# Forget and gate columns computed behind the value columns, in blocks of 344 to 358, in a two-layer decoder trunk

## The chip, the cores and the metric

The kernel runs on one core of a Trainium2 chip. The metric is device time of one execution in microseconds; the time before is the median of three runs, 2304.24 (2301.83 to 2304.35). Less is better.

## The reference, cut to what matters

A token sequence of 256 x 2048 passes through two layers in float32. Each layer normalises the residual stream, projects it with one combined matrix, runs attention, projects back, adds, and then does the same with a squared-ReLU MLP (2048 to 8192 to 2048).

```python
# layer 0: combined projection, split into
qa, ka, va, ga, fa, qd, kd, vd = split(h @ w_in)    # 1024 x 4, 8, 1024 x 3 columns
log_f = log_sigmoid(fa + b_f)                       # 8 forget columns, one for each head
o_a = fox_attention(qa, ka, va, log_f) * sigmoid(ga)
# layer 1: combined projection, split into
q, kc, vc, ks, vs, kw, vw, gt = split(h @ w_in)     # 2048, 512 x 6, 48 columns
gates = sigmoid(gt)                                 # 3 gates for each of 16 heads
kc, vc = compress(kc), compress(vc)                 # flat blocks of 32 tokens @ w1, gelu, @ w2
o = gate0 * o_cmp + gate1 * o_slc + gate2 * o_win   # three attention branches a head
```

With 256 tokens there are only four selection blocks, so the selected branch takes every block and is an ordinary causal attention.

## The kernel before, in words

Tokens lie on partitions in two halves of 128. Every float32 product is made of three matmuls: activations and weights are each split into a high and a low part, and high x high, high x low and low x high are summed in PSUM. The transposed activations xT are kept on chip in both parts; the weights are streamed.

A block of the input projection is 512 weight columns wide: `in_proj` (line 662) calls `a_units` (line 271). The 16 slices of the inner dimension come in four chunks of four (1 MB, one DMA on the SP queue; three raw buffers), and each chunk is two units of 1024 columns (two slices of 512). For each unit, ScalarE copies the high part (line 235) and VectorE subtracts to get the low part (line 236). `ahead` (line 250) writes out the split of the unit three places on, and the load of the next chunk, before each unit's matmuls; a load waits until the chunk that had its buffer is split. A unit of 512-column slices has 12 matmuls, with xT as the weights of the array and the streamed columns as the moving operand. The last unit ends with an evacuation of either half from PSUM (`plain` at line 665, or `Prep.evac` for q and k, which adds the norm).

The narrow columns, 8 forget columns in layer 0 and 48 gate columns in layer 1, have a unit of their own, `t_units` (line 363): one chunk of all 16 slices; the narrow weights are held by the array and xT moves (16 pairs of matmuls of 512 and 256 columns, lines 373 and 374). The sum is then turned by two small transposes (line 384), and `evac_fa` (line 650) or `evac_gt` (line 839) does the pointwise part.

All instructions of an engine run in the order written. The order is set by a small planner, `Background` (line 104 on): heads, norms and transposes are tasks that advance step by step in "slots", which the main matmuls offer four times a unit (`yield`; two steps at most a slot). Steps of one kind are held apart by a number of slots, also across tasks:

```python
APART = {"s": 4, "t": 3, "o": 5, "d": 3}   # scores, transposes, values, scaling
```

`bg.need(task)` runs slots with no main matmul between them until the task is done (forced slots). Three such places matter here. `phi_units` (line 863), the compression's first product, forces the task that transposes the tokens and adds position terms (`bg.need(tok[kind], ...)`, line 870; the task is started as the token block's last half is evacuated). `out_proj` (line 730) forces, unit by unit, the two heads whose rows it is to multiply (`odd_ready`, line 1039). And q and k evacuations of layer 0's dilated heads force the heads whose buffers they overwrite.

The order of blocks in layer 0 is: q, k, forget unit, v, gate (output gate) for heads 0 to 3; q, k, v, gate for heads 4 to 7; then q, k, v for each group of four dilated heads. A group's four head tasks start when its v block is evacuated. In layer 1 it is: k tokens, gate unit, phi for k (two chunks), v tokens, ks, phi for v, kw, vs, q0, vw, q1, q2, q3, output projection. A group of four heads (and its compressed-branch task `odd_comp`) starts when its q block is evacuated; each head has two "s", two "t" and one "o" step, `odd_comp` one "s" and one "t", and the preparation of q ("Prep") two "d" and three "t". A head holds two of eight score tiles.

Of the kernel before, what the change touches and what calls it, by code (L numbers as in the profile page):

```python
# [12 lines left out]
AF = mybir.ActivationFunctionType  # L13
ALU = mybir.AluOpType
AX = mybir.AxisListType

S = 256
# [130 lines left out]
def trunk_kernel(ctx: ExitStack, tc: tile.TileContext, x, w_up, w_down, even_w_in, even_w_out,  # L148
# [58 lines left out]
    def weight_chunk(w, k0, nk, segs):  # L207

        width = sum(n for _, n in segs)
        pieces, at = [], 0  # L210
        for c0, n in segs:
            src = w[k0 * 128:(k0 + nk) * 128, c0:c0 + n].rearrange("(k p) c -> p k c", p=128)
            pieces.append((nk, width, at, n, src))
            at += n
        return chunk(pieces)
# [144 lines left out]

                units.append((ci, j0 * 512, 1024, gen, True))

    def t_units(w, c0, m, rhs, evac, pre):

        ci = weight_chunk(w, 0, KT, [(c0, m)])

        def gen(u):
            pre(range(KT))
            o = rotate("main", bank[0:3])[:m]
            h = wh[u % NHL][:, :KT * m].rearrange("p (k c) -> p k c", c=m)  # L370
            lo = wl[u % NHL][:, :KT * m].rearrange("p (k c) -> p k c", c=m)
            for k in range(KT):
                nc.tensor.matmul(o, h[:, k], rhs(k), start=k == 0, stop=False)
                nc.tensor.matmul(o[:, :S], lo[:, k], rhs(k)[:, :S], start=False, stop=k == KT - 1)
                if k % 4 == 3 and k < KT - 1:
                    yield
            a, b = T[8][:m, 0:S], T[8][:m, S:2 * S]
            nc.scalar.activation(a, o[:, S:], AF.Copy)
            nc.vector.tensor_tensor(b, o[:, :S], a, ALU.add)

            def turn():
                t = rotate("tp", bank[3:5])
                for hf in range(2):
                    nc.tensor.transpose(t[:, hf * m:(hf + 1) * m], b[:, hf * 128:(hf + 1) * 128], ident[:m, :m])
                for hf in range(2):
                    evac(hf, t[:, hf * m:(hf + 1) * m])
                yield 2
            turned.append(bg.spawn(turn(), 4))
            yield

        units.append((ci, 0, KT * m, gen, True))

    turned = []


    class Norm:
        def __init__(self, name, gain):
# [59 lines left out]
    def rotate(name, of):  # L457
        rot[name] += 1
        return of[(rot[name] - 1) % len(of)]
# [202 lines left out]
    def in_proj(segs, evac, norm, nk=4):  # L662
        return a_units(W, segs, xl, list(range(KT)), evac, main3, norm.need, nk=nk)

    def plain(norm, dst, then=None):
        def evac(hf, ps):
            nc.scalar.activation(dst[:, hf * 512:(hf + 1) * 512], ps, AF.Copy, scale=norm.rows()[:, hf:hf + 1])
            if hf == 1 and then:
                then()
        return evac  # L670

    def even_head(kind, i, head, qT, kT, v, preps, gate):
        yield (lambda: all(p.task and p.task.done for p in preps) and turned[0].done and free_ht), "s"
        t = free_ht.pop(0)
        s = rotate("s", bank[5:7])
        if kind == "fox":
            scores(s, qT, kT, lambda tt, p: nlf[p][:, tt, head:head + 1].to_broadcast([128, 128]))
        else:
            scores(s, qT, kT)
        softmax(s, c_("mask") if kind == "fox" else c_("lc"), SM[t], stat[t])  # L680
        yield 8, "t"
        transposed(SM[t], SM[t])
        yield 7
        yield (lambda: gate is None or gate and gate[0].task and gate[0].task.done), "o"
        o = bank[7][:, (head % 2) * 256:(head % 2) * 256 + 256]
        values(o, v, i, SM[t], True, True)
        parts(head, o, gate and gate[0].dst[:, i * S:(i + 1) * S])
        free_ht.append(t)

    W = even_w_in  # L690
    qs = [T[0], T[1]]
    nblk = 0
    for kind, base, h0 in (("fox", 0, 0), ("dil", 4 * FOX_W + 8, 8)):
        for blk in range(2):
            qT, kT, v = (T[2], T[3], T[6]) if nblk % 2 == 0 else (T[4], T[5], T[7])
            nblk += 1
            preps = []
            for j, (dst, nm) in enumerate(((qT, "q"), (kT, "k"))):
                def evac(hf, ps, j=j, dst=dst, nm=nm, preps=preps, kind=kind, blk=blk):
                    if hf == 0:  # L700
                        n0.rows()
                        if kind == "dil":
                            bg.need(*[heads[blk * 4 + i] for i in range(4)])
                        if kind == "fox":
                            p = Prep(n0, qs[j], dst, cols["fox"] if nm == "q" else None, None)
                        else:
                            p = Prep(n0, qs[j], dst, cols[nm + "d"], rt[nm + "d"])
                        preps.append(p)
                    preps[j].evac(hf, ps)
                in_proj([(base + j * FOX_W + blk * 512, 512)], evac, n0)  # L710
            if nblk == 1:
                t_units(W, 4 * FOX_W, 8, xr, evac_fa, n0.need)

            gate = [] if kind == "fox" else None

            def then(kind=kind, blk=blk, h0=h0, qT=qT, kT=kT, v=v, preps=preps, gate=gate):
                for i in range(4):
                    head = h0 + blk * 4 + i
                    heads[head] = bg.spawn(even_head(kind, i, head, qT[:, i * S:(i + 1) * S], kT[:, i * S:(i + 1) * S], v, preps, gate), 1 + i)
            in_proj([(base + 2 * FOX_W + blk * 512, 512)], plain(n0, v, then), n0)  # L720

            if kind == "fox":
                def gate_evac(hf, ps, blk=blk, gate=gate):
                    if hf == 0:
                        gate.append(Gate(n0, qs[0], T[8 + blk]))
                    gate[0].evac(hf, ps)
                in_proj([(3 * FOX_W + blk * 512, 512)], gate_evac, n0)
# [201 lines left out]

    def odd_comp(g, qT, prep):  # L930

        yield (lambda: prep[0].task and prep[0].task.done and comp["k"].done and comp["v"].done and turned[1].done), "s"
        b = rotate("s", bank[5:7])[:, 0:128].rearrange("p (f h n) -> p f h n", f=2, h=4)
        c, st = cs, cst[g % 2]
        for hf in range(2):
            for h in range(4):
                nc.tensor.matmul(b[:, hf, h, 0:NCMP], qT[:, h * S + hf * 128:h * S + (hf + 1) * 128], kcT[:, g],
                                 start=True, stop=True, skip_group_check=True)
        cv = c[:, :, :, 0:NCMP]

        def bc(name):
            return c_(name).rearrange("p (f n) -> p f n", f=2)[:, :, None, :].to_broadcast([128, 2, 4, NCMP])

        def per(at):
            return st[:, at:at + 8].rearrange("p (f h) -> p f h", f=2)

        nc.vector.tensor_tensor(cv, b[:, :, :, 0:NCMP], bc("mc"), ALU.add)
        nc.vector.tensor_reduce(per(0), cv, AX.X, ALU.max)
        nc.vector.tensor_tensor(cv, cv, per(0)[:, :, :, None].to_broadcast([128, 2, 4, NCMP]), ALU.subtract)
        nc.scalar.activation(cv, cv, AF.Exp)  # L950
        nc.vector.tensor_tensor(cv, cv, bc("m01"), ALU.mult)
        nc.vector.tensor_reduce(per(0), cv, AX.X, ALU.add)
        nc.vector.tensor_scalar(st[:, 0:8], st[:, 0:8], 1e-30, None, op0=ALU.max)
        nc.vector.reciprocal(st[:, 0:8], st[:, 0:8])
        gt = gates.rearrange("p f (h b) -> p f h b", b=3)[:, :, 4 * g:4 * g + 4, 0]
        nc.vector.tensor_tensor(per(0), per(0), gt, ALU.mult)
        nc.vector.tensor_tensor(cv, cv, per(0)[:, :, :, None].to_broadcast([128, 2, 4, NCMP]), ALU.mult)
        yield 10, "t"
        t = rotate("tp", bank[3:5])
        for hf in range(2):  # L960
            nc.tensor.transpose(t[:, hf * 128:(hf + 1) * 128], c[:, hf].rearrange("p h n -> p (h n)"), ident)
        nc.scalar.activation(pcT[g % 2], t[:, :S], AF.Copy)
        yield 4
# [34 lines left out]
        in_proj([(c0, 512)], plain(n1, src, then), n1)  # L998

    comp_block("k", Q_W)  # L1000
    t_units(W, Q_W + 6 * KV_W, 48, xr, evac_gt, n1.need)
    phi_units("k", k_w1)
    comp_block("v", Q_W + KV_W)

# [25 lines left out]
        in_proj([(g * 512, 512)], evac, n1)  # L1030

    k_block("w", Q_W + 4 * KV_W, kwT, "okw")
    in_proj([(Q_W + 3 * KV_W, 512)], plain(n1, vs), n1)
    q_block(0)
    in_proj([(Q_W + 5 * KV_W, 512)], plain(n1, vw, lambda: vdone.append(True)), n1)
    for g in range(1, 4):
        q_block(g)

    def odd_ready(ks):
# [59 lines left out]
```

## Time and profile before

| | us |
|---|---|
| median of three runs | 2304.24 |
| profiled execution | 2303.22 |
| its span, first to last instruction | 2301.4 |
| TensorE busy | 2285.3 |
| VectorE busy | 1382.1 |
| ScalarE busy | 1086.6 |

Busy times are sums over the span; TensorE's include overlaps of matmuls that follow each other, so the cost of one is read from the start of one to the start of the next. In rows in order of time the columns are start, duration (both us), engine, line, operation, output and input tiles with their forms, and how many were merged; a square bracket at the end gives idle time before the instruction and what released it. The granted clock is TensorE's, with 1.00 as full speed.

### The profile page before, as it was taken

Reading aid. Unit: us, or ns where it says so; the run is one execution under the profiler, and the core shown is the slowest. Engines: PE = TensorE matmul, PEld = TensorE weight load, DVE = VectorE, ACT = ScalarE, POOL = GpSimd, SP = SyncE. Lnnn points to the kernel's source line nnn. Section 1 sums busy time; section 2 is a strip of 40 time slices with the busy share of each in tenths; the row PEclk is TensorE's granted clock in tenths of the full one; section 3 lists DMA queues with packets and bytes.
Section 4 is the critical chain, followed back from the end, with each engine's and each line's share of the span. In section 5 each row is a group of like instructions: output and inputs, shape, how many; then the busy total and the mean of one; then the engine's idle time right before and its main releaser. Section 6 shows DMA issues by size and latency. Waiting matters only on the chain.

```text
span 2301.4 us, 28635 instructions
## 1 busy us (share of the span) xinstructions
PE 2285.3 (99%) x11399; PEld 1922.5 (84%) x11399; DVE 1382.1 (60%) x2075; ACT 1086.6 (47%) x1573; POOL 30.0 (1%) x28
## 2 busy tenths in 40 slices
PE   8999999999999999999999999999999999999999
PEld 6788888888888888888888888788888888888887
DVE  5565655666566566566654666766666556566564
ACT  5554554544444444444443555555544444444342
POOL 0000000000000000000000000000000000000000
PEclk9999999999999999999999999999999999999999
DMA  6555555555555565565546653335555565555654
GB/s 240 165 165 171 176 165 167 181 192 193 184 198 186 188 196 183 183 201 184 188 148 204 215 165 121 118 110 174 191 186 190 181 199 193 187 193 176 203 195 148
DMA packets 212694, 414.47 MB, mean 180 GB/s; under 512 B 10705, under 2 KB 11985, under 8 KB 212561
## 3 DMA queue, kind: packets, MB, share of 16 engines
q1 hardware_dynamic: 211552, 411.53, 54.9%
q8 instruction: 89, 1.46, 0.3%
q10 hardware_dynamic: 1008, 1.12, 0.1%
q14 instruction: 45, 0.36, 0.0%
HBM read 410.52 MB, written 2.10 MB: 179 GB/s over the span
## 4 chain that ended last, share of the span: by engine, by line
PE 96%; DVE 1%; ACT 1%; DMA 1%; issue 0%; POOL 0%; ACTq 0%; POOLq 0%
PE bank L311 34%; PE bank L340 21%; PE bank L337 11%; PE bank L300 8%; PE bank L298 8%; PE bank L299 8%; PE bank L616 1%; PE bank L588 1%; PE bank L611 1%; DMA raw<-in_even_w_in 1%; PE bank L876 1%; DVE wl L236 1%; PE bank L507 1%; PE bank L617 0%; PE bank L425 0%; PE bank L584 0%
## 5 line engine op out<-in xcount | busy, mean ns | idle before, releaser
L236 DVE TENSOR_TENSOR wl<-raw,wh 128x1024 fp32r<-128x1024 f32 (+1 forms) x772 | 937.9, 1219 | 768.5 <-ACT wh L235 766.3
L235 ACT ACTIVATE wh<-raw 128x1024 fp32r<-128x1024 f32 (+1 forms) x772 | 812.3, 1054 | 864.8 <-PE bank L311 324.1
L340 PE MATMUL bank<-xT,wh 128*128 128x512 f32 x2048 | 707.6, 397 | 0.0
L337 PE MATMUL bank<-xT,wl 128*128 128x256 f32 x2048 | 543.0, 281 | 0.0
L340 PEld LDWEIGHTS bank<-xT,wh 128*128 128x128 f32 x2048 | 371.5, 188 | 75.2
L337 PEld LDWEIGHTS bank<-xT,wl 128*128 128x128 f32 x2048 | 386.6, 189 | 18.5
L311 PE MATMUL bank<-wh,big 128*128 128x512 f32 x1280 | 358.8, 391 | 0.0
L311 PE MATMUL bank<-wh,xT 128*128 128x512 f32 x1156 | 325.6, 395 | 0.8 <-ACT xT L430 0.7
L311 PEld LDWEIGHTS bank<-wh,big 128*128 128x128 f32 x1280 | 239.6, 188 | 49.3 <-DVE big L625 0.2
L298 PE MATMUL bank<-wh,big 128*128 128x512 f32 x640 | 252.8, 395 | 0.0
L311 PEld LDWEIGHTS bank<-wh,xT 128*128 128x128 f32 x1156 | 214.9, 188 | 44.6 <-ACT xT L430 1.3
L300 PE MATMUL bank<-wh,big 128*128 128x512 f32 x640 | 249.5, 390 | 0.0
L299 PE MATMUL bank<-wl,big 128*128 128x512 f32 x640 | 249.2, 389 | 0.0
L311 PE MATMUL bank<-wl,big 128*128 128x512 f32 x640 | 202.8, 393 | 0.0
L311 PE MATMUL bank<-wl,xT 128*128 128x512 f32 x578 | 188.5, 397 | 0.0
L300 PEld LDWEIGHTS bank<-wh,big 128*128 128x128 f32 x640 | 120.1, 188 | 25.7 <-DVE big L625 0.4
L298 PEld LDWEIGHTS bank<-wh,big 128*128 128x128 f32 x640 | 120.4, 188 | 24.4 <-ACT big L624 0.2
L311 PEld LDWEIGHTS bank<-wl,big 128*128 128x128 f32 x640 | 120.2, 188 | 24.5
L299 PEld LDWEIGHTS bank<-wl,big 128*128 128x128 f32 x640 | 120.4, 188 | 23.5
L311 PEld LDWEIGHTS bank<-wl,xT 128*128 128x128 f32 x578 | 108.5, 188 | 22.5 <-DVE wl L236 0.2
L787 DVE SCALAR_TENSOR_TENSOR xs<-bank,r_m,xs 128x512 f32<-128x512 f32 x128 | 89.9, 743 | 7.8 <-PE bank L300 7.8
L773 ACT ACTIVATE big<-t 128x256 fp32r<-128x256 f32 x128 | 52.5, 415 | 81.9 <-DVE t L769 81.9
(179 smaller groups left out, 1454.9 us busy)
## 6 DMA issues: line engine op xcount, KB each, us to landing
raw<-in_w_up SPq DMA_DIRECT2D x128, 1024.0 KB, 5.3
raw<-in_w_down SPq DMA_DIRECT2D x128, 1024.0 KB, 5.1
raw<-in_even_w_in SPq DMA_DIRECT2D x55, 1024.0 KB, 5.1
raw<-in_odd_w_in SPq DMA_DIRECT2D x40, 1024.0 KB, 5.1
raw<-in_even_w_out SPq DMA_DIRECT2D x16, 1024.0 KB, 5.0
raw<-in_odd_w_out SPq DMA_DIRECT2D x16, 1024.0 KB, 5.3
out_x<-xs SPq DMA_DIRECT2D x8, 256.0 KB, 2.5
xs<-in_x SPq DMA_DIRECT2D x3, 512.0 KB, 8.8
```

The costliest lines, as they stand in the source:

```text
L235: nc.scalar.activation(h, r, AF.Copy)
L236: nc.vector.tensor_tensor(lo, r, h, ALU.subtract)
L298: nc.tensor.matmul(o, lhs(k, 0, hf), h[:, n], start=st, stop=False)
L299: nc.tensor.matmul(o, lhs(k, 0, hf), lo[:, n], start=False, stop=False)
L300: nc.tensor.matmul(o, lhs(k, 1, hf), h[:, n], start=False, stop=last and n == len(ks) - 1)
L311: nc.tensor.matmul(bks[hf], lhs(k, part, hf), w_[:, n], start=False, stop=False)
L337: nc.tensor.matmul(o[:, :S], lo[:, n, j * 128:(j + 1) * 128], rhs(k)[:, :S], start=False, stop=last and n == 1)
L340: nc.tensor.matmul(o, h[:, n, j * 128:(j + 1) * 128], rhs(k), start=first and n == 0, stop=False)
L507: nc.tensor.transpose(b[:, i * S + hf * 128:i * S + hf * 128 + 128], self.src[:, hf * 512 + h * 128:hf * 512 + (h + 1) * 128], ident)
L588: nc.tensor.matmul(s[:, 128:384], qT[:, 128:256], kT, start=True, stop=bias is None, skip_group_check=True)
L773: nc.scalar.activation(d[:, k, 0], q_, AF.Copy)
L787: nc.vector.scalar_tensor_tensor(xd, ps, norm.r2[:, hf:hf + 1], xd, op0=ALU.mult, op1=ALU.add)
```

## The change

`t_units` is gone. `rows_block` takes a list of column ranges, lays them side by side, cuts the total into three blocks of equal, even width, and computes each as an ordinary block of `in_proj`. A block that spans two ranges loads each chunk in two DMAs and evacuates each piece with its own function. In layer 0 the 1024 value columns of heads 0 to 7 and the 8 forget columns make 1032, three blocks of 344; they stand behind the first k block, where the forget unit and the first v block were, and the second v block is gone from its place. Heads 0 to 3 start when the third block is evacuated, heads 4 to 7 when their k block is. In layer 1 the 512 vs, 512 vw and 48 gate columns make 1072, blocks of 358, 358 and 356; they stand where vs stood, and q0 to q3 follow one another. The gate unit between the k tokens and phi is gone.

```diff
-    def t_units(w, c0, m, rhs, evac, pre):
...
+    def rows_block(norm, sources, count, then):
+        places, n = [], 0
+        for c0, m, take in sources:
+            places.append((n, n + m, c0, take))
+            n += m
+        step = -(-n // count) + (-(-n // count)) % 2
+        for i in range(count):
+            cut = [(max(a, i * step), min(b, (i + 1) * step), a, c0, take) for a, b, c0, take in places
+                   if a < (i + 1) * step and b > i * step]
+
+            def evac(hf, ps, i=i, cut=cut):
+                for a, b, base, _, take in cut:
+                    take(hf, a - base, ps[:, a - i * step:b - i * step])
+                if hf == 1 and i == count - 1:
+                    then()
+            in_proj([(c0 + a - base, b - a) for a, b, base, c0, _ in cut], evac, norm)
+
+    def kept(norm, dst):
+        def take(hf, a, ps):
+            d = dst[:, hf * 512 + a:hf * 512 + a + ps.shape[-1]]
+            nc.scalar.activation(d, ps, AF.Copy, scale=norm.rows()[:, hf:hf + 1])
+        return take
...
+                    if hf == 1 and j == 1 and kind == "fox" and blk == 1:
+                        then()
                 in_proj([(base + j * FOX_W + blk * 512, 512)], evac, n0)
-            if nblk == 1:
-                t_units(W, 4 * FOX_W, 8, xr, evac_fa, n0.need)
...
-            in_proj([(base + 2 * FOX_W + blk * 512, 512)], plain(n0, v, then), n0)
+            if kind == "dil":
+                in_proj([(base + 2 * FOX_W + blk * 512, 512)], plain(n0, v, then), n0)
+            elif blk == 0:
+                def fa_then(then=then):
+                    fa_done.append(True)
+                    then()
+                rows_block(n0, [(2 * FOX_W, 512, kept(n0, T[6])), (2 * FOX_W + 512, 512, kept(n0, T[7])),
+                                (4 * FOX_W, 8, lambda hf, a, ps: evac_fa(hf, ps))], 3, fa_then)
...
     comp_block("k", Q_W)
-    t_units(W, Q_W + 6 * KV_W, 48, xr, evac_gt, n1.need)
     phi_units("k", k_w1)
...
     k_block("w", Q_W + 4 * KV_W, kwT, "okw")
-    in_proj([(Q_W + 3 * KV_W, 512)], plain(n1, vs), n1)
-    q_block(0)
-    in_proj([(Q_W + 5 * KV_W, 512)], plain(n1, vw, lambda: vdone.append(True)), n1)
-    for g in range(1, 4):
+    VS, VW = Q_W + 3 * KV_W, Q_W + 5 * KV_W
+    rows_block(n1, [(VS, KV_W, kept(n1, vs)), (VW, KV_W, kept(n1, vw)), (VW + KV_W, 48, lambda hf, a, ps: evac_gt(hf, ps))],
+               3, lambda: vdone.append(True))
+    for g in range(4):
         q_block(g)
```

The waits on the turned forget and gate columns (`turned[0].done`, `turned[1].done`) become waits on the third block's evacuation.

## Rows read from the trace of the kernel before

**Rows 1.** The page: busy time by engine, and the chain that ended last, by engine.
```profile
PE 2285.3 (99%) x11399; PEld 1922.5 (84%) x11399; DVE 1382.1 (60%) x2075; ACT 1086.6 (47%) x1573; POOL 30.0 (1%) x28
...
PE 96%; DVE 1%; ACT 1%; DMA 1%; issue 0%; POOL 0%; ACTq 0%; POOLq 0%
```

**Rows 2.** TensorE in order of time, around the forget unit of layer 0.
```profile
59.14 0.39 PE L299 MATMUL bank<-wl,xT 128*128 128x512 f32 x1
...
61.64 0.39 PE L373 MATMUL bank<-xT,wh 128*8 128x512 f32 x1
...
67.19 0.40 PE L298 MATMUL bank<-wh,xT 128*128 128x512 f32 x1
...
69.02 0.39 PE L300 MATMUL bank<-wh,xT 128*128 128x512 f32 x1
...
69.55 0.50 PE L298 MATMUL bank<-wh,xT 128*128 128x512 f32 x1
```

**Rows 3.** The same view, ten microseconds on: a transpose of k.
```profile
77.19 0.55 PE L507 MATMUL bank<-ident,t 128*128 128x128 f32 x3 [0.43 <-DVE t L492]
```

**Rows 4.** Groups of instructions: the splits (count, busy us, mean ns, idle before).
```profile
L236 DVE TENSOR_TENSOR wl<-raw,wh 128x1024 fp32r<-128x1024 f32 x766 | 934.0, 1224 | 765.4 <-ACT wh L235 763.3
L235 ACT ACTIVATE wh<-raw 128x1024 fp32r<-128x1024 f32 x766 | 808.9, 1058 | 863.1 <-PE bank L311 322.4 <-PE bank L340 320.9 <-PE bank L300 188.5
```

**Rows 5.** ScalarE in order of time: first forget instruction, first split behind them.
```profile
71.15 0.21 ACT L656 ACTIVATE stat<-stat 128x8 f32<-128x8 f32 x1 [2.44 <-DVE stat L654]
...
75.83 2.94 ACT L235 ACTIVATE wh<-raw 128x1024 fp32r<-128x1024 f32 x3
```

**Rows 6.** DMA issues: output, input, queue, count, KB each, median us to landing.
```profile
raw<-in_even_w_in SPq DMA_DIRECT2D x55, 1024.0 KB, 5.1
...
raw<-in_odd_w_in SPq DMA_DIRECT2D x1, 384.0 KB, 5.5
...
raw<-in_even_w_in SPq DMA_DIRECT2D x1, 64.0 KB, 5.1
```

**Rows 7.** All engines in order of time, from the k tokens' block to phi.
```profile
1189.86 21.57 SPq L227 DMA_DIRECT2D raw<-in_odd_w_in  x4
...
1195.67 0.39 PE L300 MATMUL bank<-wh,xT 128*128 128x512 f32 x1
...
1196.10 0.69 ACT L667 ACTIVATE t<-bank,r_a 128x512 f32<-128x512 f32 x1 [0.61 <-PE bank L300]
...
1197.29 0.60 PE L855 MATMUL bank<-ident,t 128*128 128x128 f32 x4
1197.64 0.47 PE L373 MATMUL bank<-xT,wh 128*48 128x512 f32 x1
...
1199.59 1.22 DVE L236 TENSOR_TENSOR wl<-raw,wh 128x1024 fp32r<-128x1024 f32 x1 [9.76 <-ACT wh L235]
...
1200.73 2.48 DVE L859 TENSOR_TENSOR t<-bank,vecs 128x512 f32<-128x512 f32 x4
...
1202.67 3.81 PE L876 MATMUL bank<-t,raw 128*128 128x60 f32 x32 [0.20 <-DVE t L859]
```

**Rows 8.** TensorE in order of time, from group 1's transposes to head 7's values.
```profile
1404.83 0.60 PE L507 MATMUL bank<-ident,t 128*128 128x128 f32 x4
...
1450.89 0.39 PE L298 MATMUL bank<-wh,big 128*128 128x512 f32 x1
...
1467.56 0.60 PE L588 MATMUL bank<-t,t 128*128 128x256 f32 x2
1470.51 0.96 PE L985 MATMUL bank<-pcT,t 128*128 128x256 f32 x2 [2.35 <-DVE big L625]
```

**Rows 9.** Stretches: busy us (count) of five engines, granted clock, DMA share, GB/s.
```profile
75.00:80.00 5.00, 4.57 (x26) 3.56 (x24) 3.98 (x7) 4.24 (x6) 0.00 (x0) 1.00 0.00 0
...
1470.00:1472.50 2.50, 1.99 (x6) 1.68 (x7) 1.66 (x10) 0.99 (x4) 0.00 (x0) 0.66 0.00 0
1472.50:1475.00 2.50, 2.50 (x12) 2.09 (x11) 0.64 (x2) 0.39 (x1) 0.00 (x0) 0.66 0.00 0
1475.00:1480.00 5.00, 5.00 (x29) 4.25 (x28) 2.77 (x10) 3.15 (x7) 0.00 (x0) 1.00 0.01 3
...
1471.00:1472.00 1.00, 1.00 (x4) 0.81 (x3) 0.20 (x3) 0.74 (x4) 0.00 (x0) 0.50 0.00 0
```

More of the change, by code (lines that the diff above doesn't have):

```diff
@@ L361, in b_units @@
                 units.append((ci, j0 * 512, 1024, gen, True))
-    def t_units(w, c0, m, rhs, evac, pre):
[L365 to L393, printed above, removed]
     class Norm:
@@ L670, in plain @@
         return evac
+    def rows_block(norm, sources, count, then):
[18 more added lines that the diff above has]
+        return take
     def even_head(kind, i, head, qT, kT, v, preps, gate):
-        yield (lambda: all(p.task and p.task.done for p in preps) and turned[0].done and free_ht), "s"
+        yield (lambda: all(p.task and p.task.done for p in preps) and fa_done and free_ht), "s"
         t = free_ht.pop(0)
@@ L692, in trunk_kernel @@
     nblk = 0
+    fa_done = []
     for kind, base, h0 in (("fox", 0, 0), ("dil", 4 * FOX_W + 8, 8)):
@@ L697, in trunk_kernel, with then, evac @@
             preps = []
+            gate = [] if kind == "fox" else None
+            def then(kind=kind, blk=blk, h0=h0, qT=qT, kT=kT, v=v, preps=preps, gate=gate):
+                for i in range(4):
+                    head = h0 + blk * 4 + i
+                    heads[head] = bg.spawn(even_head(kind, i, head, qT[:, i * S:(i + 1) * S], kT[:, i * S:(i + 1) * S], v, preps, gate), 1 + i)
             for j, (dst, nm) in enumerate(((qT, "q"), (kT, "k"))):
-                def evac(hf, ps, j=j, dst=dst, nm=nm, preps=preps, kind=kind, blk=blk):
+                def evac(hf, ps, j=j, dst=dst, nm=nm, preps=preps, kind=kind, blk=blk, then=then):
                     if hf == 0:
@@ L709, in evac @@
                     preps[j].evac(hf, ps)
+                    if hf == 1 and j == 1 and kind == "fox" and blk == 1:
+                        then()
                 in_proj([(base + j * FOX_W + blk * 512, 512)], evac, n0)
-            if nblk == 1:
-                t_units(W, 4 * FOX_W, 8, xr, evac_fa, n0.need)
[L714 to L719, printed above, removed]
-            in_proj([(base + 2 * FOX_W + blk * 512, 512)], plain(n0, v, then), n0)
+            if kind == "dil":
[6 more added lines that the diff above has]
+                                (4 * FOX_W, 8, lambda hf, a, ps: evac_fa(hf, ps))], 3, fa_then)
             if kind == "fox":
@@ L930, in odd_comp @@
     def odd_comp(g, qT, prep):
-        yield (lambda: prep[0].task and prep[0].task.done and comp["k"].done and comp["v"].done and turned[1].done), "s"
+        yield (lambda: prep[0].task and prep[0].task.done and comp["k"].done and comp["v"].done and vdone), "s"
         b = rotate("s", bank[5:7])[:, 0:128].rearrange("p (f h n) -> p f h n", f=2, h=4)
```

## The prediction

> **What bounds the kernel now.** I read the page first: the busy shares, then the chain that ended last [rows 1]. TensorE is busy for 2285.3 of 2301.4 us and carries 96% of the chain, so a microsecond is gained where a TensorE column goes, and lost where TensorE stands still. Then I read TensorE in order of time around the two column units that go (forget and gate), and last the three places where its work could come to depend on what stood around them: the first compression, the ScalarE chain behind the forget columns, and the sixteen odd heads before their output projection.
>
> What a matmul costs is read from start to start, since the durations overlap. From 59.14 to 61.64 stand 11 matmuls of 512 columns: 0.2273 us each. From 61.64 to 67.19 stand the forget unit's 16 pairs of 512 and 256 columns: 0.3469 a pair, so 0.1196 for 256 [rows 2]. A straight line through the two is 0.4207 ns a column and 0.012 us beside it: 0.1566 for 344, 0.1625 for 358, 0.1617 for 356. The bounds are the plain proportions from either side: for 344, 0.1527 (from 512) and 0.1607 (from 256).
>
> **The change part by part.**
>
> *Layer 0, columns.* Out go two value blocks of 96 matmuls (192 x 0.2273 = 43.64) and the forget unit (5.55). In come 3 x 96 matmuls of 344: 45.10 (43.98 to 46.28 by the bounds). That is -4.09. The unit's two transposes go as well (from 69.02 to 69.55 passes 0.53 where a matmul takes 0.23: -0.30), and with them a stop of 0.43 at 77.19, where a transpose waited for VectorE behind the forget arithmetic [rows 2, 3]. Together -4.8.
>
> *Layer 1, columns.* 43.64 + 5.55 + 0.30 go; 96 x (2 x 0.1625 + 0.1617) = 46.72 come (45.7 to 48.1). That is -2.8. Both: -7.6, with -9.7 and -5.0 as ends.
>
> The Trainium skill, "TensorE: Matmul & The Clock Gate", section "Back-to-back issue gap", puts the start-to-start time at columns/2.4 ns plus a fixed 2.5 ns. By it both layers' matmuls would save about 7.6 against my 6.6 from the rows alone, and the forecast below would be 1.0 lower. The rows show 227 ns for 512 columns where the rule gives 216, so I keep the rows.
>
> *Splits and evacuations.* 48 units of 688 or 716 columns replace 32 of 1024 and two small ones. A 1024-column unit takes ScalarE 1.058 and VectorE 1.224 [rows 4], beside 12 matmuls of 2.73; in proportion the narrow ones take about 0.7 and 0.85 beside 1.88 to 1.95. Cover stays, cost nothing. The forget arithmetic moves into the evacuation. Before, ScalarE was held by it from 71.15 to 75.83 [rows 5]; this now starts at the end of the third block, when three gate units of 2.73 are already split: 8.2 us plus the block's last half of 0.9, against some 6.5 for the chain and 2.3 for the next split. Cost nothing, 0.5 if it is missed.
>
> *Loads.* The pieces are narrower and most chunks have two. The 64 KB forget chunk of 2048 rows of 32 B landed in 5.1 us like a 1024 KB chunk, the 384 KB gate chunk in 5.5 [rows 6]; a quarter of these rows comes with each chunk of the third block. A chunk can be issued some eight units (15 us) before its own unit, so 6 to 7 us for two pieces are covered. The Trainium skill, "DMA: Bandwidth & Descriptors", section "Specifications", puts line rate at 512 B and more and so speaks against pieces of 32 and 192 B; by it loads would be late, which is rival D.
>
> *The first compression (layer 1).* The step that I find most costly. Before, the 48-column unit stood between the k tokens' block and the phi matmuls, and hid that the tokens must be evacuated, transposed and given their position terms. Now `phi_units` forces that task at once (line 870). Worked out on the rows of before [rows 7]: TensorE's last matmul of the block starts at 1195.67, so it is free at 1195.90; evacuation runs from 1196.10 to 1196.8, and the transposes followed it at 1197.29. Four of them passed in 0.35 (to 1197.64), so eight end at 1198.0. VectorE has the split of the second unit of the v tokens ahead of the additions: ScalarE copies after the evacuation (1196.8 to 1197.85), VectorE subtracts to 1199.1; then four additions of 0.62 (the row's 2.48), of which the phi matmuls need three: 1200.96, start at 1201.05. TensorE is idle for 1.4 + 3.0 = 4.4 us. Before it stood 0.2 at this place, so +4.2. The queue of loads adds nothing: the v tokens' first load goes out one place earlier than at 1189.86. Bounds: 1.3 if the additions came before the split and ran beside the transposes, 6 if the evacuation too is queued behind a split that waits for its load.
>
> *The clock after it.* The nearest rows: after TensorE stood still for 2.35 us before 1470.51, its granted clock was 0.50 from 1471 to 1472, the lower of its two levels (1.2 for 2.4 GHz). The two rows from 1470 to 1475 have 0.66, the next 1.00: 5 x 0.34 / 0.5 = 3.4 us at half speed, 1.7 us of work lost [rows 8, 9]. A stop of 3.0 should cost the same: +1.7 (0 to 1.7).
>
> *The odd heads.* q0 moves behind the value blocks, so vw's 32 slots no longer lie between q0 and q1. By my count of planner slots, nine steps of kind "s" a group at four slots are 36, where one block has 32. Before, group 0 had 64 slots ahead of group 1, whose q transposes began at 1404.83, behind group 0's last values. Still head 7 was late when the output projection, begun at 1450.89, asked for it: the 2.35 us before 1470.51 [rows 8]. After, group 1's transposes take turns with group 0's ("t", three slots), and its prep ends some 17 slots later. Heads 4 and 5, wanted by the projection's third unit, are then some 20 slots short, 6 and 7 a further 7. Forced slots carry head work that is needed anyway (three scores, five transposes, two heads' values: about 7 us), and ScalarE and VectorE need some 9.8 for the same steps: one more stop of about 2.5. Bounds 0 and 8.7 (below). I take +2.5, nearest to the 2.35 of the row. The last two groups run under forced slots too and so gain the room back before the second pass.
>
> *Sum*: -7.6 + 4.2 + 1.7 + 2.5 = +0.8. The profiled execution took 2303.22 (its span and 1.8 around it), so 2304.0; the median of the runs is 1.0 above that execution, which I leave out.
>
> **The rivals.** What a measurement of this kernel can tell from no change is about 0.2%, 4.6 us.
>
> A, *the columns' gain arrives*: the compression's stop is near its lower bound (1.3) and the clock does not fall, and the heads are no later than before. 2303.2 - 7.6 + 1.3 - 0.2 = 2296.7. For it: phi waited only 0.2 before, and the clock stayed at 1.00 around the stop of 0.43 [rows 9]. Against: line 870 leaves no slot between.
>
> B, *slower, by the heads' queue*: every head that the projection asks for too early is a stop like that at 1470.51, since its values wait for the evacuation of the head before. Three stops of 2.35 and a second fall of the clock, 1.7, are 8.7 instead of 2.5: 2310.2. It decides when head 5's second transposes are not out as the third projection unit starts. For it: the queue was late already by one head; against: forced slots are filled by the next heads' work.
>
> C, *the merging does not do what it says*: a 344-column matmul costs more than its share, at the upper ends: -5.0 in place of -7.6, so 2306.6, inside my forecast's own band. Nothing in the rows speaks for it but that no width between 256 and 512 stands there; against: 32 matmuls of 60 columns at 1202.67, each with a full weight load, take 3.81 together, so a load is no floor at 0.157 [rows 7].
>
> D, *late loads*: eight third-block chunks each late by a quarter of 5.1 us: +10, 2314.
>
> **How the numbers follow.** Forecast with C 0.50, A 0.24, B 0.21, D 0.05. The forecast's own range is 2299 to 2308, the terms' ends not all falling together. To hold eight in ten I go to A on one side and past B on the other: 2296.5 to 2311.5. Faster by over 0.2% is A and a little of the forecast's low end, 0.25; slower is B, D and less of its high end, 0.27; the rest, 0.48, is no change.
>
> **What would show it.** Starts of the 344-column matmuls 0.157 apart, 45.1 us for three such blocks in layer 0 and no stop where the gate block follows; a TensorE wait of about 3 us before the first phi matmul, released by the additions' line, and the granted clock at 0.5 behind it; two forced stretches at the start of layer 1's output projection, with 5 us or more of waits for VectorE or ScalarE there instead of 2.35. It is wrong if phi starts without a stop (then A), if more than 6 us are added before the projection's fourth unit (then B), or if ScalarE's copies wait for loads inside the new blocks (then D).

## The result and the profile after

The changed kernel takes 2320.83 us (median of four runs, 2319.58 to 2321.92) against 2303.98 before: 1.0075 times, 95% interval 1.0063 to 1.0087. It is slower by 17 us, and outside the range. The profiled execution took 2321.92, its span 2320.1. Line numbers below are those of the kernel shown; the lines of the changed kernel from 711 on are two higher than before's, those from 363 to 639 are 32 lower. A fence of "stretches" has the columns of [rows 9], one of grouped waits gives total, times and longest, in us.

The page, against [rows 1]: TensorE's busy sum rises by 6.6 us although columns were taken away, and it also stands still more. The page's chain of waits broke off half way (its shares sum to 48%), so it is not used.

```profile
PE 2291.9 (99%) x11523; PEld 1947.6 (84%) x11523; DVE 1383.5 (60%) x2087; ACT 1089.2 (47%) x1593; POOL 32.1 (1%) x28
```

Four milestones, read in the engine's order of time, say where the time came in:

| | before | after | stretch longer by | forecast |
|---|---|---|---|---|
| first q evacuated | 39.58 | 40.19 | 0.6 | 0 |
| q of the first dilated group evacuated | 241.11 | 243.40 | 1.7 | -4.8 |
| k tokens' last matmul, to v tokens evacuated | 1195.90 to 1233.38 | 1198.15 to 1241.49 | 5.9 | 0.1 |
| kw evacuated, to the first MLP matmul of layer 1 | 300.59 long | 311.13 long | 10.5 | 5.6 |

(The forecast's terms for the third stretch are 4.2 + 1.7 - 5.85 for the gate unit; for the fourth 2.5 + 3.1, since three blocks of 358 columns take 3.1 more than two of 512.) The sum is 18.7, as the spans show. With the gate unit's 5.85 gone, 5.9 more in the third stretch means that 11.7 came in.

TensorE's waits, grouped by who ended them, name three new families: `nlf` (the forget terms), `t` of L861 (phi), and the heads of layer 1.

```profile
PE bank L878 <- DVE t L861: 3.0, 1, 3.0
PE bank L579 <- ACT pcT L964: 2.9, 1, 2.9
PE bank L555 <- DVE nlf L627: 2.3, 1, 2.3
PE bank L579 <- ACT sm L581: 1.8, 2, 1.3
PE bank L552 <- DVE stat L566: 1.6, 1, 1.6
```

**Layer 0.** TensorE in order of time, first block, then the end of the third (against [rows 2]):

```profile
62.24 0.32 PE L298 MATMUL bank<-wh,xT 128*128 128x344 f32 x1
...
64.11 0.48 PE L311 MATMUL bank<-wh,xT 128*128 128x344 f32 x2
...
108.46 0.40 PE L298 MATMUL bank<-wh,xT 128*128 128x512 f32 x1
...
111.86 0.69 PE L555 MATMUL bank<-triu,nlf 128*128 128x128 f32 x2 [2.32 <-DVE nlf L627]
...
115.33 0.69 PE L561 MATMUL bank<-triu,nlf 128*128 128x128 f32 x2 [1.39 <-DVE nlf L627]
115.81 0.73 PE L298 MATMUL bank<-wh,xT 128*128 128x512 f32 x1
```

From the first to the end of the third block pass 46.2 us, with about one of other work between the 288 matmuls; within a unit they stand 0.156 to 0.158 apart (the first twelve pass from 62.24 to 64.11). At 111.86 the bias matmul of head 0 waits for the forget terms, and behind it, in the order written, stands the gate block, whose weights are ready. ScalarE shows why the terms are late (against [rows 5]): three table loads of 1.28 us stand in the chain. They are not new: the same three stood in the chain before, up to the 75.83 of [rows 5], where no head waited for its end.

```profile
109.67 0.21 ACT L624 ACTIVATE stat<-stat 128x8 f32<-128x8 f32 x1 [1.41 <-DVE stat L622]
109.89 1.28 ACT L625 ACT_TABLE_LOAD   x1
...
111.84 1.28 ACT L624 ACT_TABLE_LOAD   x1
...
113.36 1.28 ACT L625 ACT_TABLE_LOAD   x1
114.66 0.21 ACT L625 ACTIVATE stat<-stat 128x8 f32<-128x8 f32 x1
```

**The first compression** (against [rows 7]); TensorE in order of time, then stretches:

```profile
1199.09 0.98 PE L857 MATMUL bank<-ident,t 128*128 128x128 f32 x7 [0.67 <-ACT t L635]
1203.09 13.22 PE L878 MATMUL bank<-t,raw 128*128 128x60 f32 x64 [3.02 <-DVE t L861]
1216.08 0.78 PE L298 MATMUL bank<-wh,xT 128*128 128x512 f32 x1
...
1221.16 0.63 PE L311 MATMUL bank<-wh,xT 128*128 128x512 f32 x2
```
```profile
1202.00:1204.00 2.00, 0.91 (x8) 0.91 (x8) 1.63 (x3) 0.00 (x0) 0.00 (x0) 0.97 0.00 0
1204.00:1206.00 2.00, 2.00 (x11) 2.00 (x11) 0.00 (x0) 0.00 (x0) 0.00 (x0) 0.50 0.00 0
...
1218.00:1220.00 2.00, 2.00 (x6) 1.59 (x5) 1.34 (x3) 1.05 (x2) 0.00 (x0) 0.50 0.95 352
1220.00:1222.00 2.00, 2.00 (x8) 1.55 (x7) 0.30 (x1) 0.42 (x1) 0.00 (x0) 0.77 1.05 407
```

The stop came as forecast. But the granted clock stays at 0.50, the lower level, through all of phi and into the next block. (Phi's 64 records are 32 matmuls: two records each, as e11 shows. So the "32 matmuls of 60 columns" of the prediction's rival C are 16, and the "64 matmuls" of the expectations are 32.)

**The heads of layer 1** (against [rows 8, 9]); the stops, then stretches:

```profile
1472.20 0.49 PE L552 MATMUL bank<-t,t 128*128 128x128 f32 x2 [1.64 <-DVE stat L566]
1476.87 0.90 PE L579 MATMUL bank<-ident,sm 128*128 128x128 f32 x3 [2.94 <-ACT pcT L964]
1479.58 1.54 PE L579 MATMUL bank<-ident,sm 128*128 128x128 f32 x6 [0.53 <-ACT sm L581]
1493.00 0.70 PE L987 MATMUL bank<-pcT,t 128*128 128x256 f32 x2 [0.97 <-DVE big L593]
```
```profile
1472.00:1476.00 4.00, 1.61 (x7) 0.83 (x7) 3.03 (x15) 1.63 (x8) 0.00 (x0) 0.69 0.74 253
1476.00:1480.00 4.00, 2.60 (x9) 1.89 (x10) 2.51 (x13) 2.82 (x11) 0.00 (x0) 0.50 0.03 11
1480.00:1484.00 4.00, 4.00 (x17) 3.52 (x15) 1.56 (x9) 1.74 (x6) 0.00 (x0) 0.53 0.00 0
```

The stop of 1.3 that before had too and those shown sum to 7.4 where before had 1.3 + 2.35: 3.7 more. The clock's loss, by TensorE's busy time in these stretches, is 1.61 x 0.31 + 2.60 x 0.50 + 4.00 x 0.47 = 3.7, where by [rows 9] before lost (1.99 + 2.50) x 0.34 = 1.5: 2.2 more. That is 5.9 of the 7.4 (10.5 less 3.1 of columns). The 358 columns' own pitch, 0.164 where the forecast had 0.1625, adds some 0.4 over 288 matmuls:

```profile
1295.02 0.32 PE L298 MATMUL bank<-wh,xT 128*128 128x358 f32 x1
...
1296.99 0.48 PE L311 MATMUL bank<-wh,xT 128*128 128x358 f32 x2
```

The remaining 1.1 is not assigned.

### The profile page after: what moved, and what is told of

Same layout as the page of the kernel before. It is cut to its first block, busy times and chain, and to the rows that moved or that the text cites. A ratio compares the mean times of both kernels' runs of the same rounds, so it can differ in the third digit from the quotient of the medians.

```text
span 2320.1 us, 28980 instructions
## 1 busy us (share of the span) xinstructions
PE 2291.9 (99%) x11523; PEld 1947.6 (84%) x11523; DVE 1383.5 (60%) x2087; ACT 1089.2 (47%) x1593; POOL 32.1 (1%) x28
## 5 line engine op out<-in xcount | busy, mean ns | idle before, releaser
L236 DVE TENSOR_TENSOR wl<-raw,wh 128x1024 fp32r<-128x1024 f32 (+3 forms) x786 | 940.2, 1201 | 782.9 <-ACT wh L235 780.8
L235 ACT ACTIVATE wh<-raw 128x1024 fp32r<-128x1024 f32 (+3 forms) x786 | 815.0, 1039 | 898.8 <-PE bank L311 329.2
L311 PE MATMUL bank<-wh,xT 128*128 128x512 f32 (+3 forms) x1252 | 330.9, 378 | 1.7 <-ACT xT L398 1.6
L311 PEld LDWEIGHTS bank<-wh,xT 128*128 128x128 f32 x1252 | 227.4, 188 | 38.0 <-ACT xT L398 2.2
L311 PE MATMUL bank<-wl,xT 128*128 128x512 f32 (+3 forms) x626 | 194.2, 382 | 0.0
L311 PEld LDWEIGHTS bank<-wl,xT 128*128 128x128 f32 x626 | 115.7, 188 | 18.7 <-DVE wl L236 0.3
```

The costliest lines, as they stand in the source:

```text
L235: nc.scalar.activation(h, r, AF.Copy)
L236: nc.vector.tensor_tensor(lo, r, h, ALU.subtract)
L311: nc.tensor.matmul(bks[hf], lhs(k, part, hf), w_[:, n], start=False, stop=False)
```

## The experiments

The theory after the traces: three separate costs, each a wait at an order that the change made tight, and each made larger by the clock. Theories F (forget terms), P (phi, and the clock behind it) and Q (heads' queue). Against each stands a rival, among them that the blocks themselves are at fault (their loads, their splits, their width). Each ratio is against runs of before made beside it (medians 2303.4 for e1 to e4, 2303.2 for e5 to e7, 2302.9 for e8 and e9, 2302.3 for e10 to e12); "back" is measured from the changed kernel's 2320.8; that kernel was not run again.

**e1: forget columns first**, so that their arithmetic is done when the heads start.

```diff
-rows_block(n0, [(2 * FOX_W, 512, ..), (2 * FOX_W + 512, 512, ..), (4 * FOX_W, 8, ..evac_fa..)], 3, fa_then)
+rows_block(n0, [(4 * FOX_W, 8, ..evac_fa..), (2 * FOX_W, 512, ..), (2 * FOX_W + 512, 512, ..)], 3, fa_then)
```

> The changed kernel (2320.8), with one edit: the 8 forget columns lie ahead of the 1024 value columns, so they are in the first of the three blocks and not in the third. Same matmuls, same loads in size. Theory W (a new wait): heads 0 to 3 are started at the end of the third block, at the moment when the forget arithmetic starts, and the first head's bias matmuls stand in TensorE's queue for 2.3 and 1.4 us, with some 6.3 us at half clock behind it (3.1 lost). With the forget columns first, the arithmetic is done 30 us earlier: 6.9 us less, 2313.9, and no wait of L555 or L561 for the forget values. Rival (the forget arithmetic in the evacuation holds up ScalarE and VectorE, and so the splits): the same chain stands in the first block, the stop moves there, and the time stays within 1.5 us of 2320.8.

Measured 2315.85, 1.0053 [1.0036, 1.0069]. The waits for `nlf` are gone, and a smaller one came: the values' evacuation is queued behind the forget arithmetic and holds a PSUM bank that the next block needs.

```profile
80.43 0.42 PE L298 MATMUL bank<-wh,xT 128*128 128x344 f32 x1 [1.69 <-ACT t L662]
```

F holds: 5.0 us back, 1.7 given away again.

**e2: the ks block between the k tokens and phi for k** (and kw between the v tokens and phi for v).

```diff
-comp_block("k"); phi_units("k"); comp_block("v"); k_block("s"); phi_units("v"); k_block("w")
+comp_block("k"); k_block("s"); phi_units("k"); comp_block("v"); k_block("w"); phi_units("v")
```

> The changed kernel (2320.8), with layer 1's blocks in another order: k tokens, ks, phi for k, v tokens, kw, phi for v, so that a key block lies between each token block and its phi; nothing else. Theory P (stop and clock): phi for k no longer waits for transposes and additions (0.7 + 3.0 us), and the granted clock stays at 1.00 in both phis, so the 13.2 us of phi for k go back to 7.6 and the matmuls behind it lose 2.3 less: 11.6 us less in all, 2309.2. Rival, as I predicted it (a stop and one short fall of the clock, 1.7): 5.6 less, 2315.2. Second rival (the loads of phi set the time there): no change.

Measured 2309.86, 1.0026 [1.0015, 1.0037]: 11.0 us back of the 11.7 that P adds up to (3.7 of stops, 8.0 of clock, the latter priced by e4). Phi in TensorE's order of time has no stop and takes 7.28 in place of 13.22:

```profile
1221.84 7.28 PE L878 MATMUL bank<-t,raw 128*128 128x60 f32 x64
```

**e3: q0 ahead of the third block of layer 1**, the gates in the first; the compressed branch's condition on the third block is dropped with it.

```diff
-rows_block(n1, [vs, vw, gates], 3, ..)
-for g in range(4): q_block(g)
+rows_block(n1, [gates, vs, vw], 3, .., before={2: lambda: q_block(0)})
+for g in range(1, 4): q_block(g)
```

> The changed kernel (2320.8), with layer 1's columns in the order gate, vs, vw, and the block of q0 put ahead of the third of the three blocks, so that a block lies between q0 and q1 again, as before the change; the values still wait for the third block. Theory Q (the heads' queue): group 1's preparation no longer takes turns with group 0's, heads 4 to 7 are ready as they were before, and the stops at the start of the output projection go from some 6 us and 3.5 lost to the clock back to 2.4 to 3.6 and 1.7: 5 to 6 less, 2315. Rival (the stops there come with the later heads whatever stands between q0 and q1, or from the projection's loads): within 1.5 us of 2320.8.

Measured 2315.58, 1.0051 [1.0036, 1.0066]: 5.2 us back. The four stops are gone, and the 2.35 of before has come back in their place. Since the edit moves the gates, q0 and that condition at once, the 5.2 belongs to the order as a whole:

```profile
1481.65 0.70 PE L989 MATMUL bank<-pcT,t 128*128 128x256 f32 x2 [2.35 <-DVE big L593]
```

**e4: the wait ahead of phi filled** with 13 matmuls of 512 columns (results thrown away). It leaves the wait in place and takes away only the idleness.

```diff
 bg.need(tok[kind], *comp.values())
+for _ in range(13): nc.tensor.matmul(state["b"], xl(0, 0, 0), xr(0), start=True, stop=True)
```

> The changed kernel (2320.8), with 13 more matmuls of 512 columns (3.0 us, of xT with itself into the PSUM bank that phi starts afresh) between the transposes of the k tokens and phi's first matmul: TensorE has something to do while it waits for VectorE's additions. Nothing is taken away; the wait for VectorE is as long as it was. Theory C (the clock is most of the price): the clock stays at 1.00, phi for k takes 7.6 instead of 13.2, and the matmuls behind it lose nothing: 7.5 to 8 us less, 2313. Rival (the clock would come back within some 3.4 us, so that the 17 us at half clock have another cause, say phi itself behind a late load): 0 to 1.7 less, 2319 to 2321, or 3 more.

Measured 2314.35, 1.0047 [1.0032, 1.0062]: 6.5 us back by the medians (8.1 by the spans of the profiled executions) with no wait removed. Phi takes 7.39:

```profile
1200.68 3.23 PE L876 MATMUL bank<-xT 128*128 128x512 f32 x13
1203.95 7.39 PE L881 MATMUL bank<-t,raw 128*128 128x60 f32 x64
...
1213.97 0.62 PE L311 MATMUL bank<-wh,xT 128*128 128x512 f32 x2
```

From phi's start to the next block's 13th matmul are 10.0 us here and 18.1 in the changed kernel (1203.09 to 1221.16): the clock alone costs 8.0. (Phi starts 0.9 later here than in the changed kernel, because the fill runs past the wait, so some 7.2 of it can show in the time.)

**e5: the kernel before, with its gate unit moved behind phi for k**; no merged block at all. In this order the unit's sum shares a scratch tile with the compression, so the gates' values differ from the reference's; only its time is used.

```diff
-t_units(gates); phi_units("k")
+phi_units("k"); t_units(gates)
```

> The kernel before (2303.4), with one edit: layer 1's 48-column gate unit stands behind phi for k and not ahead of it. No column is merged; the same instructions, in another order. Theory P (what the unit was worth at its place was the cover for the transposes and additions): TensorE waits some 3.9 us ahead of phi, phi for k runs at half clock (13.2 for 7.6), and the unit behind it loses some 2 more before the clock is back: 10 to 12 slower, 2314. Rival (my prediction's price, a stop and 1.7): 2309. Second rival (merging, narrow blocks or their loads are at fault): 2303.4, no change.

Measured 2314.03, 1.0048 [1.0035, 1.0062]: 10.8 us for moving one unit. Blocks, loads and widths are those of before, so none of them is the cause of P.

```profile
1197.20 0.98 PE L855 MATMUL bank<-ident,t 128*128 128x128 f32 x7 [0.67 <-ACT t L667]
1201.20 13.91 PE L876 MATMUL bank<-t,raw 128*128 128x60 f32 x64 [3.02 <-DVE t L859]
```

**e10 and e11: why the clock stays low.** e10 leaves the stop (one phi matmul more takes it), then puts 30 matmuls of 512 columns ahead of phi. e11 fills the wait as e4 does, with 26 matmuls of phi's own kind.

```diff
+if kind == "k" and half == 0:
+    nc.tensor.matmul(o, r[:, 0], X[:, :, half:half + NCMP, 0], start=True, stop=True)
+    for _ in range(30): nc.tensor.matmul(state["b"], xl(0, 0, 0), xr(0), start=True, stop=True)
```

> The changed kernel with one phi matmul more, whose result is thrown away and which takes the 3 us wait, and behind it 30 matmuls of 512 columns (also thrown away), ahead of phi for k: 6.8 us of work added at full clock. Theory (after the stop the clock stays at 0.50 for as long as only the narrow phi matmuls follow; wide ones bring it back within about 5 us): granted clock 1.00 when phi starts, its 64 matmuls take 7.4 to 7.6 us in place of 13.2, and the whole takes 2320.8 + 6.8 + 2 - 8 = 2321.5 us. Rival (a stop of 3 us costs some 17 us of low clock whatever follows): phi starts at 0.50, its matmuls take 10 us or more, and the whole takes 2327 us or more.

> The changed kernel with 26 matmuls of phi's own kind (60 columns, results thrown away) in the wait before phi for k: as 13 matmuls of 512 columns did before, they fill the 3 us. Theory (narrow matmuls keep a clock that is up, they only don't bring it back): granted clock 1.00, phi's 64 matmuls 7.4 us, the whole 2314 us. Rival (narrow matmuls count as standing still): the clock falls, phi takes 13 us, 2321 us.

e10: 2322.58, 1.0088 [1.0074, 1.0101]; TensorE, and stretches:

```profile
1203.37 0.46 PE L878 MATMUL bank<-t,raw 128*128 128x60 f32 x2 [3.02 <-DVE t L861]
1203.61 8.70 PE L880 MATMUL bank<-xT 128*128 128x512 f32 x30
1212.15 7.28 PE L882 MATMUL bank<-t,raw 128*128 128x60 f32 x64
```
```profile
1206.00:1208.00 2.00, 2.00 (x7) 1.52 (x6) 0.00 (x0) 0.00 (x0) 0.00 (x0) 0.50 0.00 0
1208.00:1210.00 2.00, 2.00 (x10) 1.66 (x9) 0.00 (x0) 0.00 (x0) 0.00 (x0) 0.98 0.00 0
```

After the same stop the clock is up again at 1208, under the wide matmuls, and phi runs at 1.00. So 17 us of low clock are not what a stop of 3 us costs by itself; they are what it cost with phi behind it. e11: 2317.53, 1.0064 [1.0051, 1.0078], 3.5 above what was expected. The clock part held (1.00 throughout, phi 7.34 from 1207.05): the fill was mis-sized. The trace counts two records for one such matmul, so 26 take 5.91, not 3.0, and phi starts 3.1 later than in e4.

```profile
1201.30 5.91 PE L877 MATMUL bank<-raw 128*128 128x60 f32 x52
1207.05 7.34 PE L882 MATMUL bank<-t,raw 128*128 128x60 f32 x64
```

In these runs phi's matmuls kept a clock that was up (e4, e11); they did not bring back one that was down (the changed kernel, e5).

**e6 and e7: the repairs together.** e6 is e1 + e2 + e3 (values evacuated ahead of the forget arithmetic); e7 spreads q0, q1 and q2 among the three blocks of layer 1.

> The changed kernel with the three orders mended at once: forget columns first (and in its block the values evacuated ahead of the forget arithmetic, so that the next block's PSUM bank, which stood for 1.7 us in the first of these runs, comes free in time), a key block between each token block and its phi, and q0 ahead of the third block of layer 1. Theory (the three causes add up and nothing else was wrong with the merging): 6.9 + 11 + 5.3 less than 2320.8, 2297 to 2298, so 5 to 7 under the kernel before, near the 7.6 that the columns alone were to give. Rival (they share a cause, for example one clock loss counted twice, or the narrow blocks cost something of their own): 2303 or more.

> As the run with all three mended, but layer 1's three blocks are spread: first block, q0, second block, q1, third block, q2, q3. Heads 4 to 7 then have three blocks between their q and the output projection, where the kernel before had two; values still wait for the third block. Theory Q carried on (the stops at the projection's start, 1.3 + 2.4 us and 1.7 lost to the clock also in the kernel before, come from too few blocks behind q1): they go, 4 to 5 less than the run with all three, 2293. Rival (group 0 holds its score tiles until the third block is there, so group 1 starts late and is late again): 2297 or more.

e6: 2302.03, 0.9994 [0.9985, 1.0002]; e7: 2301.48, 0.9995 [0.9986, 1.0004]. Both theories missed: the waits of F, P and Q are gone, but no gain is shown, and e7 came out in its rival's range. In e6 new stops took part of it: 0.7 and 0.3 at 84.93 and 85.84, behind the forget arithmetic in the short block, and 1.7 at 1298.66, where the gates' evacuation stands behind a ScalarE split that had waited 2.69 us for its load (the last in TensorE's grouped waits):

```profile
PE bank L298 <- ACT gates L845: 1.7, 1, 1.7
```

In e7 a stop of 3.63 stands at 1476.31 in the output projection, released by VectorE's evacuation of an earlier block (`xs`, L742).

**e8 and e9.** Instead of moving the forget columns, heads 0 to 3 start twelve slots later. e8 takes the gates in the middle block, phi for k between ks and the v tokens, phi for v and kw between the first two blocks, and q0 ahead of the third. e9 has this layer 0 and before's layer 1.

```diff
-heads[head] = bg.spawn(even_head(..), 1 + i)
+heads[head] = bg.spawn(even_head(..), 1 + i + (12 if kind == "fox" and blk == 0 else 0))
```

> The change's blocks with the forget columns last, heads 0 to 3 of layer 0 started twelve slots later, phi for k between two wide matmul groups, the gates in the middle block of layer 1 and q0 ahead of the third block. Theory (the stops of the version with all three repairs, 1.0 us in layer 0 and 1.7 us in layer 1, are what is left to take): about 2298.5 us against 2303.2 before, layer 0 some 4 us shorter than before and no stop over 0.7 us on nlf, wl or gates. Rival (the columns are worth nothing once the stops are gone, or other stops take their place): 2301.5 or more, as the version with all three repairs.

> Layer 1 as before the change, with its gate unit; layer 0 merged as in the change, heads 0 to 3 started twelve slots later. Theory (layer 0's columns are worth what the pitch of the matmuls says, once no head waits for the forget arithmetic): q of dilation 0 evacuated 4 to 4.8 us earlier than before, 2298.5 to 2299.5 us. Rival (the delay doesn't take the wait away, or the heads' later start is paid at the other end of the stage): 2303 to 2305 us.

e8: 2296.19, 0.9973 [0.9963, 0.9983]. e9: 2297.28, 0.9978 [0.9969, 0.9987]. Both beat the kernel before, and both came out 1 to 2 us below what was expected. In e9 ScalarE's forget chain ends where it did in the changed kernel (114.84 against 114.87), with the same three table loads, but the first bias matmul comes 9 us into the gate block and has no stop. TensorE, then ScalarE at the first q and at the q of the first dilated group:

```profile
117.58 0.42 PE L587 MATMUL bank<-triu,nlf 128*128 128x128 f32 x2
```
```profile
40.16 0.69 ACT L478 ACTIVATE t<-bank,r_a 128x512 f32<-128x512 f32 x1
...
236.95 0.69 ACT L478 ACTIVATE t<-bank,r_a 128x512 f32<-128x512 f32 x1
```

That stretch, the second line of the table above, is 196.8 us long in e9 and in e8, against 201.5 before and 203.2 in the changed kernel. It is 4.7 and 4.8 shorter than before, what layer 0's columns were to give. In e12, which has before's layer 0, it is 201.5 again.

**e12: layer 1 of e8 with layer 0 of before.**

> Layer 0 as before the change, with its forget unit; layer 1 in the order and blocks of the version that beat both kernels (2296.2 us). Theory (layer 1's columns are worth 2.8 us, and its order takes no stop in exchange): 2300 to 2301 us against 2303 before. Rival (layer 1's columns bring nothing; the gain of that version was layer 0's alone, whose own run was 1.1 us from it): 2302.5 to 2303.5 us.

Measured 2300.97, 0.9992 [0.9983, 1.0001]: 1.4 us, which the interval does not tell from none. The trace has three small stops in layer 1 (0.70, 0.17 and 0.21, at 1237.30, 1252.52 and 1346.08) where before had 0.20 ahead of phi. With these 0.9 and the 0.4 of the wider pitch, some 1.5 would be left of the 2.8; that is a sum, not a measurement.

## Why the prediction was wrong

*Columns: right for layer 0, not shown for layer 1.* The 344-column matmuls stand 0.156 to 0.158 apart, as the line through 256 and 512 said; 358 take 0.164 against 0.1625. Layer 0's -4.8 arrives when nothing waits: its stretch is 4.7 and 4.8 shorter in e9 and e8, and e9 as a whole is 5.6 faster. Layer 1's -2.8 is 1.4 by e12's medians. The rule that the prediction set beside its rows from the Trainium skill, "TensorE: Matmul & The Clock Gate", section "Back-to-back issue gap", is there the spacing of an isolated matmul, and the section gives other figures for a stream of weight loads and matmuls. By that rule 344 columns would be an estimated 146 ns, where 156 to 158 were measured; the sum did not rest on it.

*"The forget arithmetic moves into the evacuation ... Cost nothing, 0.5 if it is missed": wrong, 6.4.* The price is that of the stretch, 203.2 in the changed kernel against 196.8 in e9. I weighed the chain on ScalarE against the next splits, and there the cover did hold: no stop of the gate block on a split is to be seen. What I didn't ask is who reads the chain's result. Heads 0 to 3 are started by the same evacuation, their bias matmuls read `nlf`, and TensorE runs in the order written: 2.3 and 1.4 us of stop, and some 2.5 lost at the low clock. e1 and e9 remove it, in two ways; e9 leaves the chain as it is and only starts the readers later.

*The first compression: right, with the clock behind it left out.* 4.4 us of stops forecast, 0.67 + 3.02 measured, released by the additions' line as said; e5 shows that the gate unit's place alone does it.

*"A stop of 3.0 should cost the same: +1.7 (0 to 1.7)": wrong, 8.0.* This is the term that was mis-sized most. I took the clock's cost from [rows 9], where wide matmuls followed the stop. Here 64 records of 60 columns followed, and the clock stayed at 0.50 until some 5 us into the next wide block. e4 prices it, e10 shows that what follows decides: there, behind the same stop, the 30 wide matmuls pass in 8.54 (1203.61 to 1212.15) where 30 x 0.2273 are 6.82, so 1.7 is lost, the figure forecast. The 1.7 was right for the work that it was read from and wrong for phi.

*The odd heads: right in kind, +2.5 against 7.4 (some 7 without the pitch).* The heads are late as rival B (8.7), which I gave 0.21, has it, but its wait is not the one seen. B's stops are values that wait for the evacuation of the head before, and that is 0.97 of the 6.1 shown; the others stand at scores (1.64) and transposes (2.94 and 0.53) of heads forced one behind the other, which waited for VectorE's and ScalarE's softmax and copies. e3 takes 5.2 back by runs. Several stops in a row also kept the clock near 0.5 for some ten microseconds.

*Rivals.* A did not come, C is refuted by the pitch. D's sign came and its price did not: ScalarE waited up to 4.20 us for loads in layer 1's blocks (up to 6.5 in the same layer before), but TensorE had no stop from it in the changed kernel; in e6 the 1.7 stands behind such a wait. The pieces of 16 and 96 KB landed in 4.0 and 4.6 us (DMA issues, columns as in [rows 6]). The Trainium skill, "DMA: Bandwidth & Descriptors", section "Specifications", which was the reason for D, asks for 512 B or more for line rate. The 16 KB in rows of 32 B took nearly as long as 1 MB; but 256 KB in rows of 2 KB took 4.0 too, so it is not shown that the rows' width is the reason.

```profile
raw<-in_even_w_in SPq DMA_DIRECT2D x4, 256.0 KB, 4.0
...
raw<-in_odd_w_in SPq DMA_DIRECT2D x4, 96.0 KB, 4.6
...
raw<-in_even_w_in SPq DMA_DIRECT2D x4, 16.0 KB, 4.0
```

The fault of the range: B's 2310.2 already holds the compression's stop and late heads, and both came. What neither a rival nor a bound covered were the two terms above, the clock behind phi (bounds 0 to 1.7, measured 8.0) and the readers of the forget terms (0 to 0.5, measured 6.4). They sit in different places, and they came together.

## What to carry to other kernels

When a small unit is merged away, ask what its 5 us stood between: here it covered a transposition chain, and taking it out brought in 11.7 us, twice what it took. For each moved result, list who reads it and what is written behind the reader on the same engine, not only what is computed beside it; delaying the readers by twelve slots turned layer 0's part from a loss of 1.7 us into a gain of 4.7. After a stop, look at what follows: here the 30 wide matmuls of e10 lost 1.7 us to the lowered clock, phi and the block behind it 8.0. A cost read behind one stop does not carry over to another with different work behind it.

## What the hardware showed that I had not expected

A stop of about 3 us lowered the granted clock to 0.50, and the clock stayed there for 13 us of 60-column matmuls with no gap between them (phi 13.22 us against 7.28 to 7.39 at 1.00), while under 512-column matmuls it was back after some 5 us (1208 in e10, 1221 in the changed kernel).

A stop of 2.35 us lowers the clock in some executions and not in others. In the profiled executions of before, e9 and e12 the clock is 0.50 behind it; in those of e3, e6 and e8 it stays at 1.00 (e12, then e8, stretches from the stop on):

```profile
1470.00:1472.00 2.00, 1.37 (x7) 1.27 (x8) 1.23 (x7) 0.99 (x4) 0.00 (x0) 0.95 0.00 0
1472.00:1474.00 2.00, 2.00 (x8) 1.63 (x7) 0.99 (x5) 0.38 (x1) 0.00 (x0) 0.50 0.00 0
```
```profile
1464.00:1466.00 2.00, 1.37 (x7) 1.27 (x8) 1.23 (x7) 0.99 (x4) 0.00 (x0) 1.00 0.00 0
1466.00:1468.00 2.00, 2.00 (x13) 1.72 (x13) 1.19 (x5) 0.56 (x2) 0.00 (x0) 1.00 0.00 0
```

The times fit this: of 18 runs of before beside e9, eight have a mean granted clock of 1.000 and a median of 2301.5, ten have 0.999 and 2303.4, which is about the 1.7 us of the prediction's clock term; that it is this stop in every one of them is not shown, since only one run of a kernel has a trace. Compared at equal mean clock (1.000, then 0.999), e9 is 4.6 and 5.4 faster than before, e8 5.5 and 5.4, and e12 1.6 and 1.5. So e8's lead over e9 is 0.9 at 1.000 and none at 0.999: layer 0's columns are the gain that is sure. What decides whether the stop lowers the clock is left open by these runs.
